# Expert stages: counts turned into integers pair by pair, one-hots behind the split of the weights' scores, and an eighteenth tile for weights

## The chip, the cores and the metric

One core of one Trainium2 chip runs the whole kernel. The metric is device microseconds of one execution; the profile is of one execution. Engines: TensorE (PE, with its weight loads PEld), VectorE (DVE), ScalarE (ACT), GpSimd (POOL) and SyncE (SP), which issues nearly all weight loads in order on one hardware queue.

## The reference, cut to what matters

Two transformer blocks run one after the other on 256 tokens of width 1024. The first has two layers (a retention and chunk-attention mixer, then a stick-breaking mixer), each followed by a mixture of experts; the second has two layers of attention, cross-attention and feed-forward. What the change touches is the mixture of experts, called twice:

```python
scores = sigmoid(t @ router_w)                       # 256 tokens, 16 experts
# best group of 4 experts by the sum of its top two, then the top two experts in it
top_w = top_s / sum(top_s)
for e in range(16):
    he = silu(t @ w_gate[e]) * (t @ w_up[e])         # 1024 -> 512
    y += combine[:, e] * (he @ w_down[e])            # 512 -> 1024
x = x + g2 * y
```

Everything is float32. Each layer's experts have 96 MB of weights (16 experts, three matrices of 2 MB).

## The kernel before, in words

`moe(l)` is one expert stage. It normalizes `x`, computes the router's scores, ranks the experts, and gets for each token and expert a place in that expert's list (`rk`) and the number of tokens of the fuller expert of each pair (`cnt`, one row of 8). Experts are worked two at a time: eight pairs p = 0 to 7, each with 64 slots per expert on the two halves of the 128 output partitions.

For the first two pairs the tokens are gathered by products with one-hot matrices (`hot`, then `gather`, results in `hg` through ACT, L1379). For pairs 2 to 7 the row numbers of the tokens are computed once (`tokens_of` builds twelve one-hot tiles on DVE, L1393; `indices` multiplies them on TensorE, L1405), and POOL fetches the rows from a copy in DRAM (`rows`, L1421) a pair or more ahead.

A pair has three products with float32 weights: `pg` (gate) and `pu` (up), L1482, then `po` (down), L1531, each 32 recorded matmuls. `up(p)` does gate and up, turns the hidden values, and prepares the rows of pair p+1; `down(p)` scales, splits in two parts (`of` L1543, `eo` L1546 and L1547) and leaves the scatter into `x` to the next pair. From pair 2 on the count is read into registers of PE, DVE and ACT (`values_load`, L1669), and two branches (L1671, L1674) skip a second part that is needed only when an expert has over 64 tokens; L1616 and L1618 do the same with the overall count for two rare paths in pairs 5 and 6.

Weights come in tiles of 1 MB: `weights()` issues four loads for each of gate, up and down of a pair, 12 a pair, 96 a stage. The tiles rotate through 17 places in a fixed order (`self.turn`, set in `phase`): two of a shared pool, five of `ring`, one shared, six of `hl`, the stage's own two (`MOE_RING`), and one of `htp`. A load waits until the products that used its place are done, and SP issues in order. At pair 7 the rotation goes back to the five `ring` tiles alone and the next mixer's first weights are asked for (`resume`).

The order of the instructions on each engine is made by a planner that simulates the program and fills an engine's idle time with whatever it takes to be ready. `tc.keep_in_program_order` (`pin`) puts an instruction behind the one traced before it on its engine; without it the planner may move it. The integer row `cnti` (L1341) is written once, before the first products; PE's register loads of all pairs need nothing else.

Of the kernel before, what the change touches and what calls it, by code (L numbers as in the profile page):

```python
# [14 lines left out]
I32 = mybir.dt.int32  # L15
AF = mybir.ActivationFunctionType
ALU = mybir.AluOpType
# [4 lines left out]
P = 128  # L22
D = 1024
S = 256
# [2 lines left out]
EPS = 1e-6  # L27
RING = 5
HL = 6
MOE_RING = 2  # L30
SHARED = 3
AHEAD = 3
PRE = 1
FIRST = 2
# [86 lines left out]
class Net:  # L121
# [1107 lines left out]
    def moe(self, l):  # L1229
        nc, I, tc = self.nc, self.I, self.tc  # L1230
        V = nc.vector
        mm = nc.tensor.matmul
        A, B = self.scale_shift(l, 1)
        with self.phase(f"moe{l}", MOE_RING, True) as mp:
# [3 lines left out]
            pin = tc.keep_in_program_order  # L1238
            rbias = self.rbias
            gate = self.gate[l, 5]  # L1240
            slots = self.k("slots")
# [93 lines left out]
            cnt = mp.tile([1, 8], F32, name="cnt")  # L1335
# [1 line left out]

            V.tensor_scalar(cnt[:, 0:FIRST], cnt[:, 0:FIRST], 32.0, None, op0=ALU.add)
            V.tensor_reduce(cnt[:, 0:1], cnt, axis=AX.X, op=ALU.max)
            cnti = mp.tile([1, 8], I32, name="cnti")  # L1340
            V.tensor_copy(cnti, cnt)  # L1341


            cs = mp.tile([P, 2, 16], F32, name="cs")
# [42 lines left out]
            def tokens_of():  # L1387
                for h in range(2):
                    for t in range(2):
                        o = self.sp.tile([P, 3, 256], BF16, tag=("e2", "gt")[h], name="ohb")  # L1390
                        e = rk[:, t, 4 + 6 * h:10 + 6 * h].rearrange("p (q j) -> p q j", j=2).unsqueeze(3)
                        for c, n, s0 in ((0, 64, 0), (128, 32, 64), (192, 32, 64)):
                            V.tensor_tensor(o[:, :, c:c + 2 * n].rearrange("p q (j s) -> p q j s", j=2),  # L1393
                                            e.to_broadcast([P, 3, 2, n]),
                                            slots[:, s0:s0 + n].unsqueeze(1).unsqueeze(1).to_broadcast([P, 3, 2, n]),
                                            op=ALU.is_equal)
                        ones_of.append(o)

            def indices():
# [67 lines left out]
            def up(p, W, between=None):  # L1467

                if p == 0:
                    oneh.extend(hot((0, 1), 0, 64))  # L1470
                    parts(1, True)
                    gather(0, 4)
                    tokens_of()
                q = slice(128 * (p % 2), 128 * (p % 2) + 128)
                pg = self.bank([P, 512], name="pg")
                pu = self.bank([P, 512], name="pu")
                for w, pp in ((W[0], pg), (W[1], pu)):
                    for k in range(KD):
                        if p == 0 and w is W[0] and k == 4:
                            gather(4, 8)  # L1480
                        for j in range(2):
                            pin(mm(pp[64 * j:64 * j + 64, :], hg[0][:, p % 2, k, 64 * j:64 * j + 64], w[j][k // 4][:, k % 4, :],  # L1482
                                   start=k == 0, stop=k == KD - 1, tile_position=(0, 64 * j)))
                if between:
                    between()
                if p == 0:
                    self.split(cs, ch, cl)
                    indices()
                hd = self.sp.tile([P, 512], F32, tag="e1", name="hd")
                nc.scalar.activation(hd, pg, AF.Silu)  # L1490
                V.tensor_tensor(hd, hd, pu, op=ALU.mult)  # L1491

                if self.pending:
                    self.pending(2)
                hidT = self.sp.tile([P, 4, P], F32, tag="e2", name="hidT")
                turn_hidden(hd, hidT)
                if self.pending:
                    self.pending(2)
                Sm, ws = places([oneh[t][:, q] for t in range(2)], p) if p < FIRST else own_places.pop(0)
                if 1 <= p < 7:  # L1500
                    columns(got[0][:, (p + 1) % 2, 0:D], P, hg[0][:, (p + 1) % 2])
                    own_places.append(known(p + 1, 0, kept[:, p % 2, :]))
                    if p < 6:
                        rows(1, p + 2)
                    if p < 5:
                        rows(0, p + 3)
                return hidT, Sm, ws
# [91 lines left out]
            engines = (mybir.EngineType.PE, mybir.EngineType.DVE, mybir.EngineType.Activation)  # L1599
# [13 lines left out]
            def rest(p, t):  # L1613


                left = nc.values_load(cnti[0:1, 0:1], min_val=0, max_val=2 * S,  # L1616
                                      engines=engines + (mybir.EngineType.Pool,))
                with tc.If(left > 96):  # L1618
                    wv = mp.tile([P, 16], F32, tag="wv", name="wv")
                    space = [e.rearrange("p a d -> p (a d)")[:, 0:2048] for e in got]  # L1620
                    hc = hg[0][:, (p + 1) % 2]
                    hid = self.sp.tile([P, 4, P], F32, tag="e1", name="hide")
                    banks = [self.bank([P, 512], name="be") for i in range(6)]
                    V.tensor_scalar(wv[:, 0:2 * FIRST], rk[:, t, 0:2 * FIRST], 64.0, None, op0=ALU.is_gt)
                    V.tensor_scalar(wv[:, 2 * FIRST:], rk[:, t, 2 * FIRST:], 96.0, None, op0=ALU.is_gt)
                    V.tensor_tensor(wv, wv, cs[:, t, :], op=ALU.mult)
                    nc.gpsimd.dma_start(space[0][:, 0:D], xd[128 * t:128 * t + 128, 0:D])
                    columns(space[0][:, 0:D], P, hc, banks[0:2])
                    n = 0

                    def fetched(src, nd):
                        nonlocal n
                        n += 1
                        return self.fetch(space[n % 2].rearrange("p (k n) -> p k n", n=nd), src, "(p k) n -> p k n", nc.gpsimd)
                    for e in range(NE):
                        for i, src in enumerate(("exp_w_gate", "exp_w_up")):
                            for b in range(2):
                                w = fetched(I[src][l, e][512 * b:512 * b + 512, :], 512)
                                for k in range(4):
                                    mm(banks[2 + i], hc[:, 4 * b + k, :], w[:, k, :], start=b + k == 0, stop=b + k == 4)  # L1640
                        hd = self.sp.tile([P, 512], F32, tag="gt", name="hde")
                        nc.scalar.activation(hd, banks[2], AF.Silu)
                        V.tensor_tensor(hd, hd, banks[3], op=ALU.mult)
                        turn_hidden(hd, hid, banks[0])
                        for b in range(2):
                            w = fetched(I["exp_w_down"][l, e][256 * b:256 * b + 256, :], D)
                            for k in range(2):
                                for c in range(2):
                                    mm(banks[4 + c], hid[:, 2 * b + k, :], w[:, k, 512 * c:512 * c + 512], start=b + k == 0,
                                       stop=b + k == 2)  # L1650
                        for c in range(2):
                            sl = slice(512 * c, 512 * c + 512)
                            of = self.sp.tile([P, 512], F32, tag="gt", name="ofe")
                            V.scalar_tensor_tensor(of, banks[4 + c], wv[:, e:e + 1], gate[:, sl], op0=ALU.mult, op1=ALU.mult)
                            V.tensor_tensor(self.x[:, t, sl], self.x[:, t, sl], of, op=ALU.add)
                    for i, q in ((0, p + 1), (1, p + 1), (0, p + 2)):
                        if q < 8:
                            rows(i, q)

            for p in range(8):  # L1660
                W = first_two(p) + [weights("exp_w_down", 256, p)]
                if p == 7:
                    self.turn, self.nload = [self.ring] * RING, 0
                    self.resume()
                if p < FIRST:
                    down(W, *up(p, W))
                    continue

                count = nc.values_load(cnti[0:1, p:p + 1], min_val=0, max_val=S, engines=engines)  # L1669
                hidT = self.sp.tile([P, 4, 64], F32, tag="e2", name="hidTb")  # L1670
                with tc.If(count > 64):  # L1671
                    Sm, ws = more_up(p, W, hidT)
                own = up(p, W, (lambda: rest(p, p - 5)) if p in (5, 6) else None)
                with tc.If(count > 64):  # L1674
                    more_down(W, hidT, Sm, ws)
                down(W, *own, p == 7)
# [789 lines left out]
```

## Time and profile before

| | |
|---|---|
| median of three runs | 1591.37 us (1589.22 to 1593.0) |
| profiled execution | 1589.33 us, its span 1587.5 us |
| PE busy | 1481.6 us, 93% of the span |
| DVE, ACT, POOL busy | 916.3, 673.7, 141.3 us |
| first expert stage, products to the last `po` | about 222 to 451 us |
| second expert stage | about 620 to 842 us |
| mean granted TensorE clock | 0.979 |

Spans and times of day below count from the first instruction of the profiled execution. The busy time of PE overstates its work, since matmuls are pipelined and each is recorded longer than its distance to the next; times between instructions are the safer reading.

### The profile page before, as it was taken

The page shows a single profiled execution, that of the slowest core. Times are in us where ns is not written, and L with a number is a line of the kernel's source. Part 1 is how long each engine was busy: PE and PEld are TensorE (multiplying, and loading weights), DVE is VectorE, ACT ScalarE, POOL GpSimd, SP SyncE. Part 2 cuts the span into 40 slices and gives each one's busy share as a digit, 9 for nine tenths or more (in the row PEclk, how much of TensorE's full clock was granted, in tenths as well). Part 3 has the DMA queues.
Part 4 walks back from the last instruction along what each step waited for, and adds up shares of the span by engine and source line. Part 5 has one row for each costly group of instructions (what it writes and reads, how often), then busy time and mean ns, then how long its engine had stood idle before and what let it go on. Part 6 is the DMA issues. An engine that isn't in the chain of part 4 may idle for free. (4 is left out here: it accounts for less than half of the span.)

```text
span 1587.5 us, 22950 instructions
## 1 busy us (share of the span) xinstructions
PE 1481.6 (93%) x8719; PEld 1043.2 (66%) x8719; DVE 916.3 (58%) x1788; ACT 673.7 (42%) x1404; POOL 141.3 (9%) x192
## 2 busy tenths in 40 slices
PE   6999969998989997999888999899999999999998
PEld 3666634334369973444335887788887997788886
DVE  4755543233269974223226776866667777766665
ACT  3434331111146543111105455665556666665554
POOL 0320001000000000100002100110001211110000
PEclk9999989999989998999999999999999999999999
DMA  9998979999967986999997541646554542546540
GB/s 357 350 314 298 355 310 419 418 418 417 412 212 249 318 322 271 419 418 417 418 417 248 149 134 67 198 161 206 192 171 152 176 144 81 190 155 205 193 159 27
DMA packets 172511, 418.14 MB, mean 263 GB/s; under 512 B 10376, under 2 KB 94016, under 8 KB 147792
## 3 DMA queue, kind: packets, MB, share of 16 engines
q1 hardware_dynamic: 165696, 403.46, 68.7%
q0 software_dynamic: 6400, 12.78, 2.4%
q8 instruction: 89, 1.46, 0.4%
q14 instruction: 54, 0.44, 0.1%
q10 hardware_dynamic: 272, 0.00, 0.0%
HBM read 422.13 MB, written 3.19 MB: 268 GB/s over the span
## 5 line engine op out<-in xcount | busy, mean ns | idle before, releaser
L230 DVE TENSOR_TENSOR hl<-w,hl 128x1024 fp32r<-128x1024 f32 x280 | 336.4, 1234 | 52.9 <-ACT hl L229 52.8
L229 ACT CAST hl<-w 128x1024 fp32r<-128x1024 f32 x280 | 280.2, 1045 | 33.5 <-DMA w<-in_even_w_in 20.5
L2341 PE MATMUL pgu<-hT,hl 128*128 128x512 f32 x640 | 224.3, 394 | 0.0
L2342 PE MATMUL pgu<-hT,hl 128*128 128x256 f32 x640 | 177.1, 277 | 0.0
L381 PE MATMUL lin<-hl,hThi 128*128 128x256 f32 (+2 forms) x480 | 159.4, 335 | 1.4 <-ACT hl L229 0.8
L382 PE MATMUL lin<-hl,hThi 128*128 128x256 f32 (+2 forms) x480 | 153.9, 321 | 2.0 <-DVE hl L230 1.9
L383 PE MATMUL lin<-hl,hTlo 128*128 128x256 f32 (+2 forms) x480 | 152.8, 320 | 0.0
L1482 PE MATMUL pg<-w,hg 128*64 128x512 f32 x512 | 120.1, 616 | 20.7 <-issue 17.0
L2341 PEld LDWEIGHTS pgu<-hT,hl 128*128 128x128 f32 x640 | 119.9, 187 | 27.8
L1491 DVE TENSOR_TENSOR hd<-hd,pu 128x512 f32<-128x512 f32 x16 | 11.0, 688 | 196.9 <-PE pu L1482 196.9
L1482 PE MATMUL pu<-w,hg 128*64 128x512 f32 x512 | 116.4, 593 | 6.0 <-DMA w<-in_exp_w_up 4.9
L2342 PEld LDWEIGHTS pgu<-hT,hl 128*128 128x128 f32 x640 | 120.2, 188 | 2.0
L1531 PE MATMUL po<-w,hidT 128*64 128x512 f32 x512 | 114.4, 599 | 6.0 <-PEq L1674 3.1
L381 PEld LDWEIGHTS lin<-hl,hThi 128*128 128x128 f32 x480 | 92.9, 194 | 16.8 <-issue 8.1
L1482 PEld LDWEIGHTS pg<-w,hg 128*64 128x64 f32 x512 | 41.6, 141 | 94.6 <-issue 78.8
L382 PEld LDWEIGHTS lin<-hl,hThi 128*128 128x128 f32 x480 | 93.0, 194 | 11.2 <-DVE hl L230 3.8
L383 PEld LDWEIGHTS lin<-hl,hTlo 128*128 128x128 f32 x480 | 92.7, 193 | 7.0 <-DVE hl L230 0.8
L1482 PEld LDWEIGHTS pu<-w,hg 128*64 128x64 f32 x512 | 41.4, 137 | 77.4 <-issue 67.0
L1531 PEld LDWEIGHTS po<-w,hidT 128*64 128x64 f32 x512 | 37.5, 138 | 72.8 <-issue 63.8
L1546 ACT CAST eo<-of 128x512 fp32r<-128x512 f32 x32 | 19.8, 617 | 132.4 <-DVE of L1543 132.2
L381 PE MATMUL linc<-hThi,hl 128*128 128x256 f32 x224 | 66.2, 296 | 0.0
L1438 ACT ACTIVATE hg<-hgT,ab 128x128 f32<-128x128 f32 x48 | 18.1, 457 | 110.3 <-PE hgT L184 110.2
(571 smaller groups left out, 2856.2 us busy)
## 6 DMA issues: line engine op xcount, KB each, us to landing
w<-in_exp_w_gate SPq DMA_DIRECT2D x64, 1024.0 KB, 17.8
w<-in_exp_w_down SPq DMA_DIRECT2D x64, 1024.0 KB, 19.8
w<-in_exp_w_up SPq DMA_DIRECT2D x64, 1024.0 KB, 17.3
w<-in_ada_w SPq DMA_DIRECT2D x48, 1024.0 KB, 7.2
w<-in_ffn_wg SPq DMA_DIRECT2D x22, 1024.0 KB, 5.5
w<-in_ffn_wu SPq DMA_DIRECT2D x22, 1024.0 KB, 7.5
w<-in_ffn_wd SPq DMA_DIRECT2D x22, 1024.0 KB, 8.9
w<-in_even_w_in SPq DMA_DIRECT2D x14, 1024.0 KB, 10.5
```

The costliest lines, as they stand in the source:

```text
L229: pin(self.nc.scalar.copy(w[:, 0], src))
L230: pin(self.nc.vector.tensor_tensor(w[:, 1], src, w[:, 0].bitcast(F32), op=ALU.subtract))
L381: pin(mm(out, lh, rh, start=start, stop=False))
L382: pin(mm(out, lh, rl, start=False, stop=False))
L383: pin(mm(out, ll, rh, start=False, stop=stop))
L1438: nc.scalar.activation(out[:, k, :], pt[:, k, :], AF.Identity, scale=self.ab[:, 0, b, k:k + 1], bias=self.ab[:, 1, b, k:k + 1])
L1482: pin(mm(pp[64 * j:64 * j + 64, :], hg[0][:, p % 2, k, 64 * j:64 * j + 64], w[j][k // 4][:, k % 4, :], start=k == 0, stop=k == KD - 1, til ...
L1491: V.tensor_tensor(hd, hd, pu, op=ALU.mult)
L1531: pin(mm(po[c][64 * j:64 * j + 64, :], hidT[:, k, 64 * j:64 * j + 64], W[2][j][k // 2][:, k % 2, 512 * c:512 * c + 512], start=k == 0, sto ...
L1546: nc.scalar.copy(eh[c], of)
L2341: mm(pp[i], wh[:, k, :], both[:, :, k, :], start=k == 0, stop=False)
L2342: mm(pp[i][:, 0, :], wl[:, k, :], hi[:, k, :], start=False, stop=k == KD - 1)
```

## The change: what it does

- `cnti`, one integer row written before the first products, becomes eight tiles of one number. Those of pairs 2 to 7 are written behind the gate and up products of the pair before, the overall count (number 0) behind those of pair 3; each is pinned on DVE. The register loads read these tiles.
- `tokens_of()` moves from before the first pair's products to behind the split of the scores (`ch`, `cl`) that follows them in program order, and its twelve DVE instructions are pinned.
- The stage's own pool of weight tiles goes from 2 to 3, so that the rotation has 18 places. Its 8 KB a partition come from the scratch for POOL's DMA descriptors, which is set to 8192 bytes a partition, half of what it was.

```diff
-MOE_RING = 2
+MOE_RING = 3
...
-            cnti = mp.tile([1, 8], I32, name="cnti")
-            V.tensor_copy(cnti, cnt)
+            number_of = {}
+
+            def count_of(*who):
+
+                for i in who:
+                    number_of[i] = mp.tile([1, 1], I32, name=f"cnti{i}")
+                    pin(V.tensor_copy(number_of[i], cnt[:, i:i + 1]))
...
-                            V.tensor_tensor(o[:, :, c:c + 2 * n].rearrange("p q (j s) -> p q j s", j=2),
+                            pin(V.tensor_tensor(o[:, :, c:c + 2 * n].rearrange("p q (j s) -> p q j s", j=2),
...
                     gather(0, 4)
-                    tokens_of()
...
+                if FIRST <= p + 1 < 8:
+                    count_of(p + 1)
+                if p == 3:
+                    count_of(0)
                 if between:
                     between()
                 if p == 0:
                     self.split(cs, ch, cl)
+                    tokens_of()
                     indices()
...
-                left = nc.values_load(cnti[0:1, 0:1], min_val=0, max_val=2 * S,
+                left = nc.values_load(number_of[0][0:1, 0:1], min_val=0, max_val=2 * S,
...
-                count = nc.values_load(cnti[0:1, p:p + 1], min_val=0, max_val=S, engines=engines)
+                count = nc.values_load(number_of[p][0:1, 0:1], min_val=0, max_val=S, engines=engines)
...
-    nc = _bacc.Bacc("TRN2", target_bir_lowering=False, num_devices=1)
+    nc = _bacc.Bacc("TRN2", target_bir_lowering=False, num_devices=1, dynamic_dma_scratch_size=8192)
```

## Rows read from the trace of the kernel before

**Rows 1.** The page: the span, and POOL's DMA queue (packets, MB, share of 16 engines).

```profile
span 1587.5 us, 22950 instructions
...
q0 software_dynamic: 6400, 12.78, 2.4%
```

**Rows 2.** Windows, first expert stage: us, busy of each engine (count), clock, DMA share, GB/s.

```profile
220.40:229.00 8.60, 6.45 (x22) 2.34 (x23) 0.00 (x0) 0.00 (x0) 0.00 (x0) 0.63 0.03 14
229.00:410.00 181.00, 169.53 (x876) 70.62 (x876) 51.09 (x87) 28.87 (x73) 12.34 (x12) 0.99 1.01 414
```

**Rows 3.** Windows, second expert stage.

```profile
615.00:628.00 13.00, 7.59 (x26) 3.14 (x27) 0.00 (x0) 0.48 (x2) 0.00 (x0) 0.61 0.10 26
628.00:816.00 188.00, 171.01 (x819) 72.21 (x819) 50.71 (x86) 26.83 (x66) 12.86 (x12) 0.98 1.01 415
```

**Rows 4.** Timeline, DVE before the first products: start, us, engine, line, operation [idle before].

```profile
210.44 2.01 DVE L1273 TENSOR_TENSOR xl<-xn,xh 128x512 fp32r<-128x512 f32 x2
212.38 2.82 DVE L1393 TENSOR_TENSOR ohb<-rk,kt 128x384 bf16<-128x384 f32 x8
...
215.20 0.17 DVE L1349 TENSOR_TENSOR cs<-cs,den 128x32 f32<-128x32 f32 x1
...
216.57 0.15 DVE L1341 CAST cnti<-cnt 1x8 int32<-1x8 f32 x1
```

**Rows 5.** Timeline, ACT in the same place.

```profile
215.40 0.22 ACT L203 CAST ch<-cs 128x32 fp32r<-128x32 f32 x1 [6.99 <-DVE cs L1349]
215.54 1.93 ACT L1379 ACTIVATE hg<-ph,ab 128x256 f32<-128x256 f32 x4
```

**Rows 6.** Timeline, PE: the end of the gather and the first gate products.

```profile
213.04 0.28 PE L1375 MATMUL ph<-kept,xl 128*128 128x256 f32 x1
222.55 5.72 PE L1482 MATMUL pg<-w,hg 128*64 128x512 f32 x16 [9.23 <-issue]
...
230.28 3.65 PE L1482 MATMUL pg<-w,hg 128*64 128x512 f32 x16
```

**Rows 7.** PE's register loads, 205 to 240 us: ns min/median/max, first and last start.

```profile
L1669 PEldq TENSOR_LOAD <-cnti x6: 299/304/487, 216.8 to 221.9; - x6
...
L1616 PEldq TENSOR_LOAD <-cnti x2: 307/308/308, 219.7 to 221.2; - x2
```

**Rows 8.** Timeline, PE at the second stage's start.

```profile
612.23 0.38 PE L1375 MATMUL ph<-kept,xl 128*128 128x256 f32 x1
620.41 6.46 PE L1482 MATMUL pg<-w,hg 128*64 128x512 f32 x16 [7.79 <-issue]
```

**Rows 9.** Timeline, PE, second stage: gate products of pairs 2 and 3.

```profile
674.17 7.09 PE L1482 MATMUL pg<-w,hg 128*64 128x512 f32 x32 [0.34 <-PEq L1671]
...
699.39 7.09 PE L1482 MATMUL pg<-w,hg 128*64 128x512 f32 x32 [0.34 <-PEq L1671]
```

**Rows 10.** Waits of PE for weights, first stage (242:456): us, times, longest.

```profile
PE pg L1482 <- DMA w<-in_exp_w_down: 0.9, 3, 0.3
```

**Rows 11.** Waits of PE for weights, second stage (642:852).

```profile
PE pu L1482 <- DMA w<-in_exp_w_up: 4.9, 4, 1.3
```

**Rows 12.** PE's branch of the rare path, first stage, and timeline of the products around it.

```profile
L1618 PEldq COMPARE_BRANCH x2: 5967/6065/6163, 380.4 to 407.6; - x2
...
382.53 2.35 PE L1482 MATMUL pu<-w,hg 128*64 128x512 f32 x10
```

**Rows 13.** Timeline, end of the first stage: last down products, next mixer's first weight split.

```profile
443.89 7.09 PE L1531 MATMUL po<-w,hidT 128*64 128x512 f32 x32 [0.30 <-PEq L1674]
...
455.98 1.03 ACT L229 CAST hl<-w 128x1024 fp32r<-128x1024 f32 x1
```

**Rows 14.** Timeline, DVE behind a pair's down products.

```profile
815.87 0.75 DVE L1543 SCALAR_TENSOR_TENSOR of<-po,ws,gate 128x512 f32<-128x512 f32 x1 [4.14 <-PE po L1531]
817.30 0.69 DVE L1547 TENSOR_TENSOR eo<-of,eo 128x512 fp32r<-128x512 f32 x1 [0.69 <-ACT eo L1546]
817.91 0.75 DVE L1543 SCALAR_TENSOR_TENSOR of<-po,ws,gate 128x512 f32<-128x512 f32 x1
```

More of the change, by code (lines that the diff above doesn't have):

```diff
@@ L1392, in tokens_of @@
                         for c, n, s0 in ((0, 64, 0), (128, 32, 64), (192, 32, 64)):
-                            V.tensor_tensor(o[:, :, c:c + 2 * n].rearrange("p q (j s) -> p q j s", j=2),
-                                            e.to_broadcast([P, 3, 2, n]),
-                                            slots[:, s0:s0 + n].unsqueeze(1).unsqueeze(1).to_broadcast([P, 3, 2, n]),
-                                            op=ALU.is_equal)
+                            pin(V.tensor_tensor(o[:, :, c:c + 2 * n].rearrange("p q (j s) -> p q j s", j=2),
+                                                e.to_broadcast([P, 3, 2, n]),
+                                                slots[:, s0:s0 + n].unsqueeze(1).unsqueeze(1).to_broadcast([P, 3, 2, n]),
+                                                op=ALU.is_equal))
                         ones_of.append(o)
```

## The prediction, made before the result was known

> **What bounds the kernel now.** I read four views in this order. The windows come first, because the change touches only the two expert stages: how much do the DMA engines move there? In the first stage they move 414 GB/s from 229 to 410 us, but 14 GB/s in the 8.6 us before [rows 2]; in the second, 415 GB/s from 628 to 816 us, and 26 GB/s in the 13 us before [rows 3]. So the weights run flat out except for one hole at the start of each stage, where all 17 places are full and no product has yet freed one.
>
> The second view is the timeline of that hole. In the first stage PE ends the gather at about 213.3 us and begins the gate products at 222.55, 9.23 us idle [rows 6]. The first 16 then take 5.72 us where the next 16 take 3.65; the granted clock in the hole is 0.63, a mix of its two levels [rows 2, 6]. The second stage has the same picture: 612.6 to 620.41, then 6.46 us [rows 8].
>
> Third, what ends the hole? Two things in series. DVE computes eight one-hots (2.82 us) ahead of `cs`, ACT has `ch` ahead of the `hg` that the products read, and `ch` waits 6.99 us for `cs`; so the first `hg` starts at 215.54 [rows 4, 5]. And PE has eight register loads ahead of the products. They wait for `cnti` at 216.57 plus 0.15 [rows 4] and run from 216.8 until the products start at 222.55 [rows 6, 7]: 5.75 us for eight, 0.72 each, although a load itself is recorded at 0.3.
>
> The fourth view says what limits the rest. In the second stage a pair takes PE 25.2 us [rows 9]; its 12 tiles of 1.049 MB take the DMA 12.6 MB / 415 GB/s = 30.3 us. PE therefore uses up its lead and waits 4.9 us for `w_up` late in the stage [rows 11]: that stage ends by its weights. In the first stage PE waits only 0.9 us for weights [rows 10], a pair having the second part there: it ends by PE.
>
> **The change part by part, first stage.** (a) Start. Without the one-hots ahead, `cs` follows `xl`: 210.44 + 2.01 + 0.17 = 212.62; `ch` with 0.22 and a hop of some 0.1 ends by 212.95; one `hg` takes about 0.5 (1.93 / 4). The products can begin at 213.5, so 222.55 - 213.5 = 9.0 us [rows 4 to 6]. If ACT takes `hg` before `ch` it is 0.2 more. What is late next is `hg`, four in 1.93 us beside 3.65 us of products, so PE itself.
>
> (b) Clock. Busy until 213.3 and again at 213.5, PE should keep the upper level: 5.72 - 3.65 = 2.1 us [rows 6]; at the lower level it is 0. I take 2.1, the clock having been at the upper level when the gather ended (0.28 us a matmul against 0.38 in the second stage [rows 6, 8]).
>
> (c) The loads do not vanish: eight are spread over pairs 2 to 6. With an empty queue they cost 0.72 each, 5.75 together [rows 7]; at best nothing, among matmuls already handed to the array. The nearest row for the latter: the branch of pair 5 occupies PE's sequencer from 380.4 for 5.97 us, yet the products run on until 382.53 + 2.35 = 384.9, 4.5 us of it covered [rows 12]. I take 1.0 us, nearer to the covered end.
>
> [...]
>
> (d) Seven conversions of 0.15 us [rows 4] replace one, on a DVE that is busy 51 of 181 us here [rows 2]: nothing. The one cover that matters is that each is done before PE's sequencer reaches its load; without it see the second rival. (e) The twelve one-hots (about 4.2 us at 0.35) run behind `cl` while DVE has nothing else until the first products end; their readers come behind the first up products. Nothing. (f) Eighteenth tile: PE ends this stage, so nothing.
>
> (g) Handover. The rotation of 18 puts the last pair's down weights on four `ring` tiles, which the next mixer's first loads need. They come free halfway through and at the end of `po`, 447.4 and 451.0, plus 2.5 us for a tile at 415 GB/s and some latency: 450 to 454 against the first split at 455.98 [rows 13]. Nothing; at most 3 us a stage if the second half decides. (h) Half the descriptor scratch: POOL's queue moves 12.78 MB in 6400 packets, 2.4% of the DMA engines' span [rows 1]. Nothing; had its service doubled, 38 us would be added to transfers spread over the whole kernel, most of it covered. I see no gain from it.
>
> Sum of the first stage: 9.0 + 2.1 - 1.0 = 10.1 us; bounds 3.3 (no clock, loads exposed) and 11.3.
>
> **Second stage.** PE's part is 620.41 - 612.65 = 7.8 at the start (there the gather's end decides), and 6.46 - 3.65 = 2.8 by the clock, 10.6 [rows 6, 8]. But the weights end this stage, so the hole in them is the gain: 13 us x (1 - 26/415) = 12.2 [rows 3]. To close it, loads must go on: the old 17 tiles last until about 615.0, the new one for 2.5 us more, 617.5; the first places come free at 612.65 + 3.65 = 616.3, or at 619.1 at the lower clock. So the hole is 0 to 2 us; I take 12.0. PE can follow: 10.6 plus the 4.9 us that it now waits [rows 11] is 15.5; with all eight loads exposed it is 9.8, the lower bound.
>
> **Sum.** 10.1 + 12.0 = 22.1 us, bounds 13.1 to 23.5. The profiled execution has 1589.33 us, 1.8 us around its span, and lies 2.0 below the median of the runs, 1591.37. Nothing after the stages waits for the DMA engines at their full rate, so it arrives at the end: 1567.2 on the profiled execution, 1569.3 on the median. I predict 1569.
>
> **The rivals.** *Loads exposed.* The planner puts each load where its simulation has PE waiting, which on the chip is where the queue is empty; 0.72 each. For it: that is what it did before [rows 7]. Against: rows 12. First stage 10.1 - 4.75 = 5.4, second 9.8: 15.2 us, 1576.
>
> *Conversions late (slower).* Place: PE's queue at the start of each pair. A conversion is pinned behind the DVE work of the pair before, whose last is the second `eo`. If PE's load stands ahead of the pair's gate products, it waits for that: the second `of` starts at 817.91 and its `eo` ends as the first did, 817.30 + 0.69 - 815.87 = 2.12 us later [rows 14]; with 0.15 and 0.72 it is 3.0 us a pair. Twelve pairs: 18 us in the first stage; in the second 18 less the 15.5 - 12.0 = 3.5 us that PE has to spare, 14.5. Net -22.1 + 32.5 = 10 slower, 1601. It decides from (22.1 + 3.5) / 12 = 2.1 us a pair. Against: gate products that are ready go first by trace order, and a load found ready behind them is found so on the chip too.
>
> *Start unmoved.* Something else on PE, ACT or DVE, placed by the planner into the same idle time, holds the first products as long; only the extra tile works, 2.5 us, and in the second stage alone: 1589. Against: the two holders seen both go, and nothing else lies between them in rows 4 to 6.
>
> **How the numbers follow.** Forecast 0.68 (own range 1563 to 1574, from the bounds of b and of the hole, and 2 us of spread of the runs), loads exposed 0.18 (1572 to 1580), start unmoved 0.06, conversions late 0.08. Under 0.2%, 3.2 us, counts as no change. Faster 0.86, same 0.06, slower 0.08. The range 1562 to 1583 takes in the forecast and the first rival; the others and the tails of both, about 0.2, stay out.
>
> **What would show it.** Right: PE idle under 1 us between gather and first gate products in both stages; first 16 products near 3.65 us in the first; `hg` starting before 213; no window of 2 us below 300 GB/s from 205 to 240 or 600 to 640 of the new timeline; single register loads among the later pairs' products; PE waiting for weights in the second stage, little in the first; first stage about 10 us shorter, second about 12. Wrong: a pair that takes over 26 us with PE idle at its load (loads exposed or conversions late), a hole in the DMA of over 3 us, or a next mixer whose first split comes later than 5 us after the last `po`.

## The result, and the profile after

The changed kernel takes 1566.03 us (median of four runs, 1564.3 to 1567.53), the kernel before beside it 1590.46 (four runs): ratio 0.9844, 95% interval 0.9827 to 0.9861, 24.4 us less. Timed once more, later, with a second profile: 1569.28 against 1591.57, ratio 0.9852 (0.9832 to 0.9871), 22.3 us less. The forecast was 1569, 22.1 us less.

The page after (to be read against [rows 1]):

```profile
span 1565.7 us, 22964 instructions
...
q0 software_dynamic: 6400, 12.78, 2.5%
```

The profiled executions differ by 1587.5 - 1565.7 = 21.8 us. Windows of both stages' starts and of what follows them (columns as in [rows 2]):

```profile
206.00:214.50 8.50, 6.56 (x35) 4.12 (x35) 7.73 (x32) 2.47 (x4) 0.34 (x1) 0.89 1.02 426
214.50:223.00 8.50, 8.50 (x47) 4.96 (x47) 4.38 (x15) 4.02 (x9) 0.74 (x1) 0.91 1.01 423
...
594.00:607.00 13.00, 10.68 (x63) 5.89 (x65) 12.23 (x44) 4.66 (x9) 1.34 (x2) 1.00 1.02 427
607.00:795.00 188.00, 174.08 (x834) 75.56 (x832) 53.16 (x96) 26.84 (x66) 12.59 (x12) 0.98 1.01 419
```

The hole in the weights (14 and 26 GB/s in [rows 2, 3]) is gone. Timeline of DVE, then of ACT, in the first stage:

```profile
212.03 2.01 DVE L1273 TENSOR_TENSOR xl<-xn,xh 128x512 fp32r<-128x512 f32 x2
...
214.04 0.17 DVE L1354 TENSOR_TENSOR cs<-cs,den 128x32 f32<-128x32 f32 x1
...
214.60 4.11 DVE L1398 TENSOR_TENSOR ohb<-rk,kt 128x384 bf16<-128x384 f32 x12
```

```profile
214.24 0.22 ACT L203 CAST ch<-cs 128x32 fp32r<-128x32 f32 x1 [4.24 <-DVE cs L1354]
214.64 1.02 ACT L1384 ACTIVATE hg<-ph,ab 128x256 f32<-128x256 f32 x2 [0.17 <-PE ph L1380]
```

`cs` follows `xl` directly and the one-hots stand behind it. PE, end of the gather and first gate products of both stages, and of the first stage in the second profile:

```profile
215.84 0.40 PE L1380 MATMUL ph<-kept,xl 128*128 128x256 f32 x1
216.17 3.65 PE L1486 MATMUL pg<-w,hg 128*64 128x512 f32 x16
...
603.83 0.28 PE L1380 MATMUL ph<-kept,xl 128*128 128x256 f32 x1
604.44 3.65 PE L1486 MATMUL pg<-w,hg 128*64 128x512 f32 x16 [0.33 <-ACT hg L1384]
...
213.96 0.28 PE L1380 MATMUL ph<-kept,xl 128*128 128x256 f32 x1
214.41 1.94 PE L1486 MATMUL pg<-w,hg 128*64 128x512 f32 x8 [0.17 <-ACT hg L1384]
```

(The second profile's window ends behind eight of its 16 products.)

The clock of the day shifts by a microsecond or two between runs, so from here times count from `pick` (DVE, L1320: 208.82 and 606.80 before, 210.41 and 599.60 after), the last common step ahead of the change. By that the first products start 13.73 us after it before and 5.76 after in the first stage, 13.61 and 4.84 in the second; in the second profile (`pick` at 209.74 and 598.54) 4.67 and 4.60. The last `po` comes 8.8 us sooner in the first stage and 14.0 in the second; the stretches outside the stages agree to 0.6 us, but for 1.6 us more ahead of the first `pick`: 8.8 + 14.0 + 0.6 - 1.6 = 21.8.

The conversions and PE's register loads of the first stage (ns min/median/max, first and last start):

```profile
L1346 DVE CAST cnti<-cnt x7: 131/142/143, 244.4 to 247.5; 1x1 int32<-1x1 f32 x7
...
L1678 PEldq TENSOR_LOAD <-cnti x6: 298/304/502, 252.0 to 257.5; - x6
...
L1625 PEldq TENSOR_LOAD <-cnti x2: 298/300/301, 255.0 to 256.8; - x2
```

All of them stand in pair 1, not spread over pairs 2 to 6. The seven conversions, too, which the change writes behind the products of pairs 1 to 6, follow one another there, behind pair 0's last DVE work: the pins did not keep them in their pairs. Waits of PE in the second stage (620:830; against [rows 11]). Here "issue" is time in which PE waits for nothing that the profile shows:

```profile
PE py L1528 <- issue: 3.6, 1, 3.6
...
PE pu L1486 <- DMA w<-in_exp_w_up: 1.1, 1, 1.1
```

The handover (against [rows 13]) keeps its 12.1 us from the start of the last `po` to the first split:

```profile
436.71 7.09 PE L1540 MATMUL po<-w,hidT 128*64 128x512 f32 x32 [0.30 <-PEq L1683]
...
448.79 1.03 ACT L229 CAST hl<-w 128x1024 fp32r<-128x1024 f32 x1
```

### The profile page after: what moved, and what is told of

The parts are those of the page before. It is cut to its first block, busy times and chain, and to the rows that moved or that the text cites. A ratio compares the mean times of both kernels' runs of the same rounds, so it can differ in the third digit from the quotient of the medians.

```text
span 1565.7 us, 22964 instructions
## 1 busy us (share of the span) xinstructions
PE 1480.8 (95%) x8719; PEld 1046.1 (67%) x8719; DVE 918.6 (59%) x1800; ACT 674.0 (43%) x1404; POOL 141.2 (9%) x192
## 3 DMA queue, kind: packets, MB, share of 16 engines
q8 instruction: 88, 1.44, 0.4%
## 5 line engine op out<-in xcount | busy, mean ns | idle before, releaser
L1486 PE MATMUL pg<-w,hg 128*64 128x512 f32 x512 | 113.7, 595 | 3.9 <-PEq L1680 3.6
L381 PEld LDWEIGHTS lin<-hl,hThi 128*128 128x128 f32 x480 | 92.9, 194 | 17.4 <-issue 8.1
```

The source lines that it names most:

```text
L381: pin(mm(out, lh, rh, start=start, stop=False))
```

## The experiments

The theory: two holders in series, `hg` behind the one-hots and PE's loads behind `cnti`, kept the first products; with both gone the hole closes. The rivals: one part does it alone, or the tile does.

**The counts alone.**

```diff
-            cnti = mp.tile([1, 8], I32, name="cnti")
-            V.tensor_copy(cnti, cnt)
+            number_of = {}
...
+                    pin(V.tensor_copy(number_of[i], cnt[:, i:i + 1]))
...
+                if FIRST <= p + 1 < 8:
+                    count_of(p + 1)
+                if p == 3:
+                    count_of(0)
...
```

> Kernel before with the counts made integers pair by pair alone (one-hots and 17 tiles as before). Theory A, two holders in series (one-hots hold hg until 215.5, register loads hold PE until 222.5): products start when the first hg is done, 6.4 us earlier in each stage instead of the 8.0 and 8.7 of the full change, and 2 to 2.8 us more by the clock; total 15 to 18 us faster. Theory B, the loads alone hold the start: all of the start's gain, 20 to 24 us. Theory C, the extra tile makes the gain: under 4 us.

1574.28 us, ratio 0.9889 (0.987 to 0.9908), 16.7 less, as expected. The first products, both stages:

```profile
216.41 5.35 PE L1487 MATMUL pg<-w,hg 128*64 128x512 f32 x16 [2.83 <-ACT hg L1384]
...
607.81 3.65 PE L1487 MATMUL pg<-w,hg 128*64 128x512 f32 x16 [2.83 <-ACT hg L1384]
```

With the loads gone, `hg` ends the wait: 7.3 us behind `pick`. The clock came back in the second stage only (3.65 us for 16 products, 5.35 in the first), behind the same wait of 2.83 us.

**The one-hots alone.**

```diff
-                            V.tensor_tensor(o[:, :, c:c + 2 * n]...
+                            pin(V.tensor_tensor(o[:, :, c:c + 2 * n]...
...
-                    tokens_of()
...
                     self.split(cs, ch, cl)
+                    tokens_of()
```

> Kernel before with the one-hots moved and pinned alone; the integer row is then made at once behind cs, and PE's eight loads still stand ahead of the products. Theory A: loads run from about 213.4 to 219 us, products start 3 to 3.5 us earlier in the first stage, 2 in the second, lower clock kept; total 5 to 6 us faster. Theory B: the same or less, since the loads decide. Theory C: no change.

1580.48 us, ratio 0.9927 (0.9911 to 0.9943), 10.5 less: more than expected. The profiled spans differ by 7.7 (1579.8 against 1587.5), the last `po` coming 2.9 and 4.6 us sooner. The rest of the 10.5 is no gain that the traces show: the profiled execution of this kernel took 1.1 us more than its median, that of the kernel before 1.6 less than the median of the 17 runs beside it.

```profile
220.23 6.45 PE L1481 MATMUL pg<-w,hg 128*64 128x512 f32 x16 [5.21 <-issue]
...
613.54 6.07 PE L1481 MATMUL pg<-w,hg 128*64 128x512 f32 x16 [5.04 <-issue]
```

Now the loads are the holder: eight of them start between 214.46 and 219.56 us in the first stage, and the first products come 9.7 and 9.6 us behind `pick`. The clock is lost as before: 6.45 and 6.07 us for the first 16.

**Both, without the tile.**

```diff
-MOE_RING = 3
+MOE_RING = 2
...
-    nc = _bacc.Bacc("TRN2", target_bir_lowering=False, num_devices=1, dynamic_dma_scratch_size=8192)
+    nc = _bacc.Bacc("TRN2", target_bir_lowering=False, num_devices=1)
```

> The changed kernel with 17 tiles and the whole scratch: counts and one-hots alone. Theory A: first stage as with the tile; in the second the hole in the weights is 2 to 3 us instead of none, worth at most 2.5 us where PE waits for weights; 22 to 24 us faster than before. Theory C: under 10 us faster.

1570.94 us, ratio 0.9863 (0.9844 to 0.9883), 20.0 less: short of the 22 to 24 expected. The start is that of the full change (4.8 and 5.8 us behind `pick`), but in the second stage a rest of the hole stays, 4 us at 154 instead of some 420 GB/s, 2.5 us of transfer, as expected:

```profile
606.00:610.00 4.00, 4.00 (x28) 2.48 (x26) 0.84 (x4) 0.94 (x2) 0.00 (x0) 1.00 0.51 154
```

**Tile and halved scratch alone**, and **the halved scratch alone** (the last line of the edit by itself).

```diff
-MOE_RING = 2
+MOE_RING = 3
...
-    nc = _bacc.Bacc("TRN2", target_bir_lowering=False, num_devices=1)
+    nc = _bacc.Bacc("TRN2", target_bir_lowering=False, num_devices=1, dynamic_dma_scratch_size=8192)
```

> Kernel before with the eighteenth tile and half the scratch alone. Theory A: the start of the products does not move; the hole in the weights shrinks by 2.5 us in both stages, which only the second stage can use; 0 to 2.5 us faster. Theory C: most of the gain, over 15 us faster. If half the scratch costs POOL anything, slower.

> The kernel before with half the descriptor scratch and nothing else. Theory A (the scratch costs and gains nothing; the 3.2 us of the tile alone are the tile's): within 1.5 us of the kernel before, 1589 to 1592. Theory B (the scratch itself moves the time, by the gather and scatter DMAs of POOL): 2 us or more to either side.

1587.73 us, ratio 0.998 (0.9967 to 0.9993), 3.2 less where up to 2.5 was expected, and 1590.03, ratio 0.999 (0.9981 to 0.9999), 1.5 less. The two intervals overlap, so the times alone do not tell the tile from the scratch; the traces do, in part: with the tile the second stage's last `po` comes 2.7 us sooner against `pick`, with the scratch alone 0.2 later. The first products do not move (13.7 and 13.6 us behind `pick`) with the tile; its hole in the second stage only begins later, at 618:

```profile
614.00:618.00 4.00, 0.00 (x0) 0.00 (x0) 0.91 (x5) 1.57 (x4) 0.51 (x1) 0.57 0.88 368
618.00:628.00 10.00, 7.49 (x31) 3.50 (x32) 0.00 (x0) 0.56 (x2) 0.00 (x0) 0.66 0.07 12
```

**The change without the pins on the one-hots.**

```diff
-                            pin(V.tensor_tensor(o[:, :, c:c + 2 * n]...
+                            V.tensor_tensor(o[:, :, c:c + 2 * n]...
```

> The changed kernel with the pins taken off the twelve one-hots: the planner then puts eight of them ahead of `cs` on DVE again; the orders of PE, ACT, POOL and SP are those of the changed kernel. Theory A (the moved one-hots alone would not have done it, the pin does; without it the start is held by the one-hots as in the run with the counts alone): first gate products about 7.3 us behind `pick` in both stages instead of 4.8 to 5.8, the weights' hole opens by 1 to 2 us, and the time is 1569 to 1572 us, 3 to 6 above the changed kernel, a gain of 19 to 22 over the kernel before. Theory B (the place in program order suffices): within 1.5 us of the changed kernel, 1565 to 1567.

1573.64 us, ratio 0.989 (0.9872 to 0.9907), 17.4 less than before: 5 to 7 us of the 22.3 to 24.4 are gone, and the interval lies just above both of the changed kernel's. The time is above the 1569 to 1572 expected. The one-hots are ahead of `cs` again, and here the pause costs the clock in both stages (with the counts alone the same pause cost it in the first only). DVE, then PE in both stages:

```profile
214.00 2.82 DVE L1398 TENSOR_TENSOR ohb<-rk,kt 128x384 bf16<-128x384 f32 x8
216.82 0.17 DVE L1354 TENSOR_TENSOR cs<-cs,den 128x32 f32<-128x32 f32 x1
...
217.79 5.02 PE L1486 MATMUL pg<-w,hg 128*64 128x512 f32 x16 [2.83 <-ACT hg L1384]
...
608.95 5.35 PE L1486 MATMUL pg<-w,hg 128*64 128x512 f32 x16 [2.84 <-ACT hg L1384]
```

Against `pick`, the second 16 begin 2.96 us later than in the first profile of the changed kernel in the first stage, 4.18 in the second: 7.1.

**One conversion in place of seven.**

```diff
-                for i in who:
-                    number_of[i] = mp.tile([1, 1], I32, name=f"cnti{i}")
-                    pin(V.tensor_copy(number_of[i], cnt[:, i:i + 1]))
+                cnti = mp.tile([1, 8], I32, name="cnti")
+                pin(V.tensor_copy(cnti, cnt))
...
-                if FIRST <= p + 1 < 8:
-                    count_of(p + 1)
-                if p == 3:
-                    count_of(0)
+                if p == 1:
+                    count_of()
```

> The changed kernel with one conversion of all eight counts, pinned behind pair 1's products, in place of the seven single ones; PE's order of instructions is unchanged by that. Theory A (what matters is that PE's loads find nothing to read before the first products are under way; doing it pair by pair does nothing, since all eight loads are issued in pair 1 anyway): within 1.5 us of the changed kernel, 1564.5 to 1567.5, and loads at the same place. Theory B (the spread over the pairs is worth something, by keeping loads or conversions out of pair 1): pair 1 longer by several tenths up to 5 us a stage, 1568 to 1576.

1566.78 us, ratio 0.9853 (0.9835 to 0.987): that of the changed kernel. Doing it pair by pair is worth nothing.

**Eight warming products.**

```diff
-WARM = (5, 3, 12, 4)
+WARM = (5, 3, 12, 8)
```

> The changed kernel with eight instead of four warming products ahead of the gather. Theory A (the first stage's start missed the forecast by 1.1 us because the clock had fallen to its lower level in the gather; more warming keeps it up): gather matmuls of 0.28 us in both stages, first gate products 4.8 us behind `pick` in both, 0.9 us off the first stage, nothing in the second: 1564.5 to 1566 us. Theory B (the level is down to chance from run to run, or the warming delays the count products on PE): no change or up to 2 us slower, 1566 to 1568.

1568.28 us, ratio 0.9856 (0.9841 to 0.9871): no gain. The gather ran at the upper clock here (0.28 us a product, granted 1.00 from 211 to 215), but so it did in the second profile of the changed kernel with four (1.00 there too). So the number of warming products does not decide it; what let the clock fall in the first profile, no run here shows.

**PE's loads doubled.**

```diff
                 count = nc.values_load(number_of[p][0:1, 0:1], ..., engines=engines)
+                nc.values_load(number_of[p][0:1, 0:1], ..., engines=(mybir.EngineType.PE,))
```

> The changed kernel with every PE register load of a pair's count issued twice (six more in each stage, twelve in all). Theory A (behind the first products a load runs in the sequencer beside products already queued and costs nothing): within 1.5 us of the changed kernel, 1564.5 to 1567.5. Theory B (a load costs its 0.72 us there too, as it did with an empty queue): 12 x 0.72 = 8.6 us more, 1573 to 1576. In between, the prediction's 1.0 us for eight loads would give 1.5 us more.

1563.23 us (1561.25 to 1566.77), ratio 0.9832 (0.9815 to 0.9849): the loads cost nothing, but no theory had it faster. In its trace the 3.6 us of "issue" in the second stage is missing. That stall stands in pair 6, among the eight scatter products `py`, in every kernel shown above; in the changed one:

```profile
780.31 0.48 PE L1527 MATMUL py<-eo,kept 128*128 128x512 f32 x1 [2.85 <-PEq L1627]
...
785.79 0.39 PE L1528 MATMUL py<-eo,kept 128*128 128x512 f32 x1 [3.59 <-issue]
```

The new theory: PE waits there for a piece of its own program. The page has a queue that it calls instruction, and in the 2 us windows from 776, 782 and 788 one packet of it starts in each; first the page, then the window 782:784:

```profile
q8 instruction: 88, 1.44, 0.4%
```

```profile
q8 instruction: 1, 0.02, 3.4%
```

1.44 MB / 88 is 16.4 KB a packet. The times of the packets in the trace fit: this one runs from 783.38 to 784.48, and PE goes on 1.3 us later; in all twelve profiles with the stall one lands during it, 1.2 to 1.5 us before PE goes on. If so, the stall has a fixed place in the program, and each instruction added ahead moves it forward. Two kernels with added loads in the first stage only (three instructions each), and the changed kernel again:

```diff
+                for again in range(1 if l == 0 else 0):   # 2 in the other
+                    nc.values_load(number_of[p][0:1, 0:1], ..., engines=(mybir.EngineType.PE,))
```

> The changed kernel with PE's loads of the pairs' counts issued twice in the first expert stage only: six loads, some 18 instructions of PE more ahead of the second stage. Theory A (the place of the stall is fixed by the number of instructions ahead of it): it stands some three scatter products earlier, at the second or third of the eight in pair 6 as in the run with eight warming products (16 instructions more), is 4 to 5 us long, and the time is that of the changed kernel or up to 2 us more, 1566 to 1568.5. Theory B (doubled loads help by themselves): about half the gain of the run with twelve loads doubled, 1564 to 1565.

> The changed kernel with PE's loads of the pairs' counts issued three times in the first expert stage only: twelve loads more, some 36 instructions of PE, all of them in pair 1 of that stage; PE's order is otherwise unchanged. Theory A (the stall of PE by 3.6 us among the scatter products of the second stage's pair 6 is the arrival of the next block of PE's program, which the trace shows as packets of 0.02 MB on an instruction queue; its place is fixed by the number of instructions ahead, so 36 more put it ahead of the taken branch L1627, where PE waits anyway): the stall is gone, pair 6 of the second stage takes about 33 instead of 35 us, the loads themselves cost nothing, and the time is 1562 to 1564.5 us, 2 to 4 below the changed kernel. Theory B (the run with doubled loads gained by chance or by its other order of loads in the second stage): 1565 to 1568. Theory C (a load costs 0.72 us in pair 1 when more of them stand together): 8.6 us more in the first stage, 1570 to 1575.

> The changed kernel once more, beside the kernels of this call: 1565 to 1568 us, 23.5 to 25.5 below the kernel before; the stall of PE in the second stage's pair 6 again at the sixth scatter product and 3 to 4 us long, if its place is fixed by the program and not by chance.

The stall in the changed kernel again (sixth product), with eight warming products (16 instructions more; third) and with six loads more (18; second):

```profile
785.96 0.59 PE L1528 MATMUL py<-eo,kept 128*128 128x512 f32 x1 [2.76 <-issue]
```

```profile
785.36 0.76 PE L1527 MATMUL py<-eo,kept 128*128 128x512 f32 x1 [4.82 <-issue]
```

```profile
786.39 0.80 PE L1528 MATMUL py<-eo,kept 128*128 128x512 f32 x1 [5.01 <-issue]
```

With 36 more it is gone, as with doubled loads, whose 36 lie in both stages. A count of the traces says the same: in all twelve profiles with the stall, 8416 to 8419 records of PE (products, weight loads, instructions of the sequencer) stand ahead of the product that waits, be it the second or the seventh; with 36 more, 8433 stand ahead of the first product behind the branch L1627, so that the place lies ahead of that branch. So it is set by the count of instructions: shown. That what arrives is the program is inferred from the queue's name, its packets and when they land.

The time of the first stage's twelve loads more is nevertheless 1571.15 us, ratio 0.9865 (0.9844 to 0.9886), that of six 1569.97, 0.9858 (0.9841 to 0.9875), the changed kernel's 1569.28 beside them. All three are above what was expected of them (theory A for the first two; 1565 to 1568 for the last), and their intervals overlap. From `pick` to the start of the last `po` in the second stage the twelve save 4.1 us against the changed kernel there (212.1 against 216.3), and lose 4.2 in the first (230.1 against 225.9), where new stalls stand:

```profile
PE pg L1486 <- PEq L1682: 3.0, 5, 1.7
...
PE hgT L184 <- issue: 1.3, 1, 1.3
PE po L1540 <- issue: 0.9, 1, 0.9
```

So theory A was right on the stall and wrong on the time; theory C's 1570 to 1575 holds the time, but its mechanism does not: it had 8.6 us lost in the first stage. The 1.7 us stand at the branch ahead of pair 2 (0.34 in the changed kernel). Sixteen of the twenty loads stand ahead of that branch, the last at 265.83, and the branch comes at 266.51, when the down products of pair 1 have ended (265.36). That the loads have used up the sequencer's lead over the products is the author's reading of these times; no run tested it. The two stalls of "issue" end 1.4 us after a packet of the same queue, which fits the program again, at new places; no run moved them. The doubled loads gave the lowest median of all; its interval overlaps that of the changed kernel, so a better version is not shown.

## Why the prediction was right

- *What holds the start*: right. Either holder alone keeps it at 7.3 or 9.6 us behind `pick`; with both gone it is 4.6 to 5.8.
- *(a) 9.0 us.* Measured 8.0 in the first profile, because most of the gather ran at the lower clock (0.41 us a product instead of 0.28, granted 0.58 in the window below); 9.1 in the second, where the clock stayed up. Second stage 8.8 and 9.0. The windows of the gather in the first and the second profile:

```profile
212.00:216.00 4.00, 3.34 (x16) 3.04 (x14) 3.72 (x11) 1.24 (x3) 0.74 (x1) 0.58 1.03 426
...
211.30:215.30 4.00, 3.17 (x20) 2.15 (x21) 3.72 (x11) 1.72 (x5) 0.73 (x1) 1.00 1.02 424
```

- *(b) 2.1 us.* Right: 3.65 us for the first 16, also in the first profile, where the premise (the clock at its upper level when the gather ends) did not hold and the clock rose only as the products began (0.50 from 214 to 216, 0.98 from 216 to 218).
- *(c) 1.0 us.* Cost right to a microsecond, place wrong: all eight loads are in pair 1, from 252.0 to 257.5, beside its up and scatter products, and cost nothing; pair 1's gate products to its `po` take 18.01 us before and after. Six more cost nothing either: from pair 0's `po` to pair 2's 50.17 us with and without them; twelve more cost 1.6, not 8.6. Ahead of the first products eight cost 5.75 us [rows 7].
- *(d), (e), (f) first stage, (g), (h)*: nothing each, as predicted: one conversion does as well as seven; the one-hots run while DVE has nothing else; the tile alone moves the first stage's last `po` by 0.6 us the wrong way; the handover is 12.1 us as before; the scratch gains 1.5 us at most. But (e) hangs on the pin, 5 to 7 us, which the prediction had not named.
- *First stage, 10.1 us.* Measured 8.8: (a) with (b) is 1.1 short and (c) 1.0 better, and pair 3 lost 1.5 us: its second part took 8.5 us for 64 products, where the granted clock (0.62 from 295 to 299, a mix of 0.50 and 1.00, the two levels it has in this execution) fell behind the same 1.9 us wait for `hga` that the kernel before has at 1.00. With one conversion the clock stayed at 1.00 there (7.07 us for the 64), and the stage gained 10.7. In the second profile of the changed kernel they took 8.77 us; with twelve loads more, the stretch from pair 2's `po` to pair 5's scatter products is 2.0 us shorter than there (94.55 against 96.53). What decides it is open. Before, then after:

```profile
303.46 7.07 PE L1566 MATMUL pgu<-w,hga 128*32 128x512 f32 x64 [1.90 <-ACT hga L1438]
...
295.02 8.53 PE L1575 MATMUL pgu<-w,hga 128*32 128x512 f32 x64 [1.90 <-ACT hga L1443]
```

- *Second stage, 12.0 us.* Measured 14.0 in the first profile, 11.6 in the second, 13.3 with one conversion. The hole closed as worked out; what spreads is the end of the stage, where waits for `w_up` and the stall at pair 6 add up to 4.7 and 6.7 us (before: 4.9 + 2.85). The prediction did not see that stall, which stood in the kernel before as well.
- *The sum, 22.1 us.* Measured 21.8 on the first profile. That it is so near is partly luck: the first stage fell 1.3 short and the second gained 2.0 more than forecast, by terms that the prediction does not have or that differ from run to run (the clock in the gather and in pair 3; the stall and the waits for `w_up` late in the second stage).
- *The rivals.* Loads exposed falls with (c); its 4.75 us are the 5.75 of [rows 7] less the 1.0 of (c). Conversions late falls: the last conversion starts at 247.5, the first load at 252.0. Start unmoved falls with the first rows after.

The gains do not add up: 16.7 and 10.5 for the parts alone, 20.0 together. In the first stage the first products move by 6.4 and 4.0 us for the parts alone, by 8.9 for both: behind each holder the next one is late. The tile with the halved scratch takes 3.2 off alone; on top of the other two parts it is 2 to 4, which is not clear of noise, since the intervals without it (0.9844 to 0.9883) and with it (0.9827 to 0.9861) overlap.

## What to carry to other kernels

Where a start waits for several things in series, look up what is late next behind each of them before pricing one: here the one-hots, left ahead of `cs`, kept 3 us of 20 with 17 places for weights, and 5 to 7 of 22 to 24 with 18. An instruction moved out of the way must be pinned there if a planner fills idle time, or it comes back. And register loads here were free beside the products of pair 1, with up to fourteen a stage, and cost 0.72 us each ahead of the first products: moving them is enough.

## What the runs showed of the hardware

PE stalled for 1.8 to 5.0 us with nothing to wait for in the profile, at a place fixed by the count of instructions ahead (8416 to 8419 records of PE in twelve profiles); it stood ahead of the second to seventh product behind the branch that skips a long body (L1627, before L1618), with the weights' queue at 100% of the DMA engines (100.2% from 780 to 786 us in the changed kernel, 99.1% from 804.6 to 807.4 in the kernel before). Each time a packet of 16.4 KB on the instruction queue landed 1.2 to 1.5 us before PE went on. That PE waits for this packet, and that it carries PE's program, is the author's inference; no run shows it directly. At that branch itself PE waited 2.6 and 2.9 us in pairs 5 and 6 of the second stage of the changed kernel, and again a packet of that queue landed in each wait, 1.8 and 1.7 us before its end.

The granted clock differed between runs of the same program in the same place: 0.58 and 1.00 in the first stage's gather, worth 1.1 us at the start. Behind one wait of 1.9 us in pair 3 it differed between kernels whose products there are the same: 1.00 in the kernel before, 0.62 in the changed one, worth 1.5 us.
